# Another issuing queue for the MLP's right factors, and the last product's splits moved into the last chunk

## The chip, the cores and the metric

The kernel runs on one core of a Trainium2 chip. The metric is the device time of one execution in microseconds; of three executions the median counts.

## The reference, cut to what matters

The program is one step of a two-layer decoder trunk for 1024 prompt tokens and 8 single sample tokens (1032 columns), with width 1024 and an MLP width of 2816. Layer 0 mixes with GLA and NSA heads, layer 1 with an mLSTM; after either mixer comes the MLP, which is what the change is about:

```
for l in range(DEPTH):
    xp, xs = xp + mixer(rmsnorm(xp)), xs + mixer(rmsnorm(xs))
    # _conv_ffn(rmsnorm(x), w_up, conv_w, conv_b, w_down, conv_state):
    #   gate, inner = split(x @ w_up)             (1024 -> 2 x 2816)
    #   gate = causal depthwise conv of width 3 over gate, + bias
    #   d = (gelu_tanh(gate) * inner) @ w_down    (2816 -> 1024)
    xp, cv = xp + conv_ffn(xp), last two gate columns
    xs, cv = xs + conv_ffn(xs), the same with the state
y_prompt, y_sample = rmsnorm(xp), rmsnorm(xs)
```

All of it is float32.

## The kernel before, in words

**Products.** TensorE multiplies float32 operands as three products of halves: a high part (the value rounded to the engine's short float, ScalarE's copy) and a low part (the difference, VectorE's subtraction). A "split" below is this pair of instructions. The MLP saves multiplications by a scheme of 7 block products in place of 8: the left operand (weights) and the right operand (activations) are each combined into seven factors, and the seven results are added into four quarters. `seven` (L536) runs one such set; product `i` of a set is followed by `after(i, ...)`, which evicts it from its PSUM bank (`ppa`, `ppb`, `ppc` in turn).

**Left factors.** `factors` (L468) makes the seven left factors of a set: two weight loads issued on SyncE's queue (SP, L473), sums on GpSimd (POOL, L477 to L497), and per factor a high part and a PSUM copy on ScalarE (ACT, L485, L487) and a low part on VectorE (DVE, L488). `fill` keeps four factors made ahead of TensorE.

**Up-projection** (`climb`). 22 hidden blocks `f` of 128 columns; each is one `seven` of 24 matmuls a product. The evictions, convolution, GELU and gate of a block run on ScalarE, VectorE and GpSimd during the next blocks. Two neighbouring blocks are a pair, the right operand of the down-projection. When a pair is complete, `turn(f, i)` splits its seven combinations, one at a time (L738 high, next step L741 low), in two staging buffers in turn (named `st` and `big`; for layer 0's last pair slots 26 and 27, `s`), and a store (L742, SyncE's queue) of 516 KB sends each to the DRAM tile `hid`. A staging buffer is refilled when its store has landed.

**Down-projection** (`descend`). The pairs are taken in chunks: layer 0 has 11 pairs, in chunks of 2, 2, 2, 2 and 3; layer 1 has nine, in 2, 2, 2 and 3. A chunk runs four block rows `j`, each one `seven` of 12 matmuls a product (18 for three pairs). The chunk's right factors, seven per pair, come back from `hid` into slots (buffers `xh`, `xl`, `s`) by `load_factors` (L624), issued on ScalarE's queue: chunk 0's behind the first four products of the last up-projection block (L777 to L779), the next chunk's at the head of each `j` (L815), a third pair's at L828. In the last chunks the stored residual rows `res` come back on SyncE's queue (L839), are scaled (L841) and added (L843) by GpSimd. The rows themselves are stored by `out_project` (L419), on SyncE's queue, before the MLP begins.

**Last product.** Layer 1's pairs cover only blocks 0 to 17. Blocks 18 to 21 go unsplit to the DRAM tile `raw` (L712) and are multiplied plainly by `finish` (L888, matmuls at L902) after the last chunk: lines 598 to 612 load eight weight slices of 256 KB, split them (L273, L274 into `fh`, `fl`), load the four rows (L608) and split them (L609, L610), and then `finish` starts. It also makes the final norm and stores the results.

**What sets the order.** `plan(at, late, step)` puts a piece of work behind product number `at` of the whole run (`late` 0 is ahead of that step's `fill`, 1 behind it). `ordered` (L522) then holds TensorE, VectorE, ScalarE and GpSimd to the order in which the program emits their instructions, between the start of the up- and the end of the down-projection; SyncE is not among them. What is outside it, SyncE's DMAs included, is put in its queue by a planner, by its own estimate of when buffers come free. Each queue runs in its order, so an instruction that waits holds what is behind it.

Of the kernel before, what the change touches and what calls it, by code (L numbers as in the profile page):

```python
# [21 lines left out]
TT = T + NS  # L22
# [49 lines left out]
class Trunk:  # L72
# [304 lines left out]
    def out_project(self, l, w, split, ks, ready, late, nat=None):  # L377


        nc = self.nc  # L380
        with self.tp(name="opp", bufs=2, space=PSUM) as pp, \
                self.tp(name="opm", bufs=2, space=PSUM) as self.ps:
            oh, ol = [None] * KD, [None] * KD

            def parts(ids):
                for i in ids:
                    oh[i], ol[i] = split(ks[i])

            def begin(m):
                wt = self.split_w([(0, w[:, m * 128:(m + 1) * 128])], KD, nat=nat)  # L390
                pt = pp.tile([128, NG, 512], F32, name="pp")
                return pt, self.product_steps([pt[:, g, :GW] for g in range(NG)], wt, oh, ol, ks)

            parts(range(2))
            split2 = self.split
            parts(range(2, ready))
            head = [begin(PAIRS[0])]
            self.take(head[0][1], ready)
            head.append(begin(PAIRS[1]))
            for _ in range(ready):  # L400
                with self.tc.issue_after(split2):
                    next(late, None)
                self.take(head[1][1], 1)
            for _ in late:
                pass
            parts(range(ready, KD))
            self.res = self.dram.tile([KD, 128, TT], F32, name="res")
            self.right = [None] * 28
            for n, m in enumerate(PAIRS):
                pt, steps = head[n] if n < 2 else begin(m)  # L410
                self.take(steps, KD)
                x = self.rstd if n % 2 else self.vec.tile([128, TT], F32, name="sq_t")
                nc.gpsimd.tensor_tensor(x, self.xh[m].bitcast(F32), self.xl[m].bitcast(F32), op=OP.add)
                for g in ((slice(1, 3), slice(0, 1)) if n == KD - 1 else (slice(0, 3),)):
                    c = slice(g.start * GW, g.stop * GW)
                    v = x[:, c].rearrange("p (g t) -> p g t", t=GW)
                    nc.vector.tensor_tensor(v, pt[:, g, :GW], v, op=OP.add)
                    nc.scalar.activation(self.big[:, m, c], x[:, c], AF.Copy, scale=self.gains[:, 16 + 8 * l + m:17 + 8 * l + m])
                nc.sync.dma_start(self.res[m], x)  # L419
                nc.scalar.activation(x, x, AF.Square)  # L420
                self.add_sq(x, n)
                if n % 2:
                    self.prepare(n // 2)
# [145 lines left out]
    def ffn(self, l, last):  # L569
# [22 lines left out]
        with self.tp(name="fpp", bufs=1, space=PSUM) as pp, self.tp(name="fpm", bufs=2, space=PSUM) as self.ps:  # L592
            self.agenda, self.step = defaultdict(list), 0
            with self.ordered():
                self.climb(l, stream, pp, right, tu, chunks, hid, raw, NP)
                self.descend(l, last, stream, pp, tu, chunks, hid)
            assert not self.agenda
        while pools:
            pools.pop().__exit__(None, None, None)
        if last:  # L600
            with self.tp(name="fin", bufs=1) as fin:
                free = [self.slot(i).rearrange("p a q w -> p (a q w)") for i in (1, 3, 5, 7, 9, 11, 13)]
                wts = [self.last_weight(w_dn[18 * 128:], 4, m, fin) for m in range(KD)[::-1]][::-1]
                y, parts = [x.bitcast(F32) for x in free[:4]], free[4:]
                while len(parts) < 8:
                    parts.insert(3, fin.tile([128, TT], F32R, name=f"o{len(parts)}"))
                for k in range(4):
                    nc.sync.dma_start(y[k], raw[k])  # L608
                    nc.scalar.activation(parts[k], y[k], AF.Copy)  # L609
                    nc.vector.tensor_tensor(parts[4 + k], y[k], parts[k], op=OP.subtract)  # L610
                with self.tp(name="flp", bufs=8, space=PSUM) as self.ps:
                    self.finish(wts, parts[:4], parts[4:], y)
        else:
            self.open_x()
            self.order = PAIRS
            for n, m in enumerate(PAIRS):
# [4 lines left out]
                    nc.scalar.activation(x, big[:, PAIRS[n + 4]], AF.Square)  # L621
                    nc.vector.tensor_tensor(self.sq, self.sq, x, op=OP.add)

    def load_factors(self, p, at, hid, ids, eng):  # L624

        for i in ids:
            x = self.slot(at + 2 * i)
            eng.dma_start(x.bitcast(F32), hid[p, i])
            self.down[p, i] = x

    def climb(self, l, stream, pp, right, tmp, chunks, hid, raw, pairs):
# [17 lines left out]
        def up(f):  # L649
# [72 lines left out]
            if f >= 2 * pairs:  # L722
                self.plan(s + (4 if wide else 8), 0, keep)
            if f % 2 and f < 2 * pairs:
                for i, n in enumerate((5, 7, 9, 11, 12, 13, 14) if wide else (10, 12, 14, 16, 17, 18, 19)):
                    self.plan(s + n, 1, lambda i=i: turn(f, i))
            return after

# [2 lines left out]
        def turn(f, i):  # L731
# [7 lines left out]

            def low():  # L740
                v.tensor_tensor(to[:, 1, :, :QW], part, to[:, 0, :, :QW], op=OP.subtract)  # L741
                nc.sync.dma_start(hid[f // 2, MADE[i]], to.bitcast(F32))  # L742
                if i in (0, 2):
                    self.sums(1 if i == 0 else 4, src, p)
            self.plan(self.step + 1, 0, low)
# [26 lines left out]
        for f in range(NF):  # L772
            done = up(f)

            def after(i, pt):
                done(i, pt)
                if f == NF - 1 and i < 4:  # L777
                    for n, c in enumerate(chunks[0]):
                        self.load_factors(c, n, hid, range(2 * i, min(2 * i + 2, 7)), nc.scalar)  # L779

            self.seven(pp, stream, lambda i: right[4 * i:4 * i + 4], after)
        self.plan(self.step + 3, 1, lambda: self.conv_store(l, cvp, cvs, rows))

    def descend(self, l, last, stream, pp, tmp, chunks, hid):

        nc, big, v, p = self.nc, self.big, self.nc.vector, self.nc.gpsimd
        st = self.st.bitcast(F32).rearrange("p a q w -> p (a q w)")
# [20 lines left out]

        for c, chunk in enumerate(chunks):
            to_go = len(chunks) - 1 - c  # L810
            loads = [(x, 14 * (1 - c % 2) + n) for n, x in enumerate(chunks[c + 1][:2])] if to_go else []
            for j in range(4):
                a11, a12, a21, a22 = (x for m in (j, j + 4) for x in (big[:, m, :HW], big[:, m, HW:]))
                t = first[j]
                for x in loads:  # L815
                    self.load_factors(*x, hid, range(2 * j, min(2 * j + 2, 7)), nc.scalar)

                def after(i, pt):
                    to, k = ((t, None), (a12, None), (a22, None), (a11, left), (a22, right), (a12, right), (a21, left))[i]
# [5 lines left out]
                        x = (a22, a12, a21)[i]  # L825
                        p.tensor_tensor(x, x, t, op=OP.add)
                    if to_go == 1 and j == 3:
                        self.load_factors(chunks[-1][2], 14 * (c % 2), hid, (i,), nc.scalar)  # L828
# [38 lines left out]
    def conv_store(self, l, cvp, cvs, rows):  # L867
# [15 lines left out]
    def last_weight(self, w, n, m, pool):  # L883

        return self.part_w(self.load_w([(0, w[:, m * 128:(m + 1) * 128])], n),
                           to=[pool.tile([128, n, 128], F32R, name=f"{x}{m}") for x in ("fh", "fl")])

    def finish(self, wts, hh, hl, ys):  # L888

# [1430 lines left out]
```

## Time and profile before

| | |
|---|---|
| median of three runs | 2863.44 us (2860.78 to 2866.82) |
| profiled execution | 2869.35 us, its span 2867.6 us |
| mean granted TensorE clock | 0.973 of full speed |
| TensorE matmul | busy 2729.6 us, 95% of the span |
| VectorE, ScalarE, GpSimd | busy 64%, 47%, 38% |
| DMA | 341.51 MB, mean 119 GB/s; SyncE's queue has 24.2% of the sixteen engines' time, ScalarE's 7.7% |
| `hid` stores | 140 of 516 KB on SyncE's queue; as many loads on ScalarE's |

The up-projection of layer 0 runs to about 1350 us of the span, its down-projection from there on; layer 1's up-projection ends at about 2575, its last chunk begins at about 2717 and ends at 2786. In a row such as `ACT st L738 ... [6.67 <-DMA hid<-st]` the bracket is the idle time of the engine in front of the instruction and what ended it. `PE` is TensorE, `DVE` VectorE, `ACT` ScalarE, `POOL` GpSimd, `SP` SyncE; a `q` behind an engine's name is its sequencer issuing DMAs. A DMA share of 1 means that all sixteen DMA engines are busy.

### The profile page before, as it was taken

The page shows a single profiled execution, that of the slowest core. Times are in us where ns is not written, and L with a number is a line of the kernel's source. Part 1 is how long each engine was busy: PE and PEld are TensorE (multiplying, and loading weights), DVE is VectorE, ACT ScalarE, POOL GpSimd, SP SyncE. Part 2 cuts the span into 40 slices and gives each one's busy share as a digit, 9 for nine tenths or more (in the row PEclk, how much of TensorE's full clock was granted, in tenths as well). Part 3 has the DMA queues.
Part 4 walks back from the last instruction along what each step waited for, and adds up shares of the span by engine and source line. Part 5 has one row for each costly group of instructions (what it writes and reads, how often), then busy time and mean ns, then how long its engine had stood idle before and what let it go on. Part 6 is the DMA issues. An engine that isn't in the chain of part 4 may idle for free.

```text
span 2867.6 us, 49399 instructions
## 1 busy us (share of the span) xinstructions
PE 2729.6 (95%) x19507; PEld 2480.6 (87%) x19507; DVE 1846.7 (64%) x3080; ACT 1338.2 (47%) x2543; POOL 1093.7 (38%) x1025
## 2 busy tenths in 40 slices
PE   7999999999998999999899999999989999999988
PEld 7886544787798999999899889889989999999987
DVE  6556675447576777776576754444767777865664
ACT  4343444334345566665544422323455666645433
POOL 3531233331143455554375311110334545445713
PEclk9999999999898999999999999999999999999999
DMA  6620100541122334446785212221223343457711
GB/s 182 185 76 12 59 0 17 183 155 37 36 79 63 111 141 141 146 144 216 282 279 188 53 37 61 61 68 47 82 63 109 136 147 135 156 211 273 281 41 71
DMA packets 298347, 341.51 MB, mean 119 GB/s; under 512 B 33741, under 2 KB 245812, under 8 KB 298052
## 3 DMA queue, kind: packets, MB, share of 16 engines
q1 hardware_dynamic: 263356, 223.48, 24.2%
q10 hardware_dynamic: 25032, 81.32, 7.7%
q0 software_dynamic: 9728, 33.56, 3.4%
q8 instruction: 154, 2.52, 0.4%
q14 instruction: 77, 0.63, 0.1%
HBM read 240.56 MB, written 101.92 MB: 119 GB/s over the span
## 4 chain that ended last, share of the span: by engine, by line
PE 82%; DVE 7%; DMA 3%; ACT 3%; issue 2%; POOL 2%; ACTq 0%; SPq 0%; DVEq 0%; POOLq 0%
PE ppb L555 18%; PE ps L285 14%; PE ppa L555 11%; PE ppc L555 11%; PE pp L285 6%; PE ps L1425 2%; PE pd L285 2%; PE ps L902 2%; PE pd L1334 1%; PE ps L1182 1%; PE pd L1400 1%; PE ps L1170 1%; PE pd L1401 1%; PE ps L1580 1%; DMA wr<-in_ffn_w_down_dram 1%
## 5 line engine op out<-in xcount | busy, mean ns | idle before, releaser
L488 DVE TENSOR_TENSOR wh<-ps,wh 128x512 fp32r<-128x512 f32 (+2 forms) x280 | 162.3, 580 | 147.5 <-ACT ps L487 144.2
L488 DVE TENSOR_TENSOR wl<-ps,wl 128x512 fp32r<-128x512 f32 (+2 forms) x280 | 162.0, 578 | 100.9 <-ACT ps L487 97.5
L285 PE MATMUL ps<-xh,wh 128*128 128x344 f32 x960 | 223.9, 338 | 0.0
L285 PE MATMUL ps<-xl,wh 128*128 128x344 f32 x960 | 216.3, 329 | 4.4 <-DVE xl L188 2.5
L272 POOL TENSOR_TENSOR wr<-wr,gains 128x1024 f32<-128x1024 f32 (+1 forms) x44 | 85.0, 1933 | 335.0 <-DMA wr<-in_odd_w_in_dram 197.9
L285 PE MATMUL ps<-xh,wl 128*128 128x344 f32 x960 | 211.9, 326 | 0.0
L487 ACT COPY ps<-wr 128x512 f32<-128x512 f32 (+2 forms) x400 | 198.7, 497 | 7.6 <-DVE st L754 6.9
L555 PE MATMUL ppb<-s,wh 128*128 128x258 f32 x1380 | 183.5, 288 | 12.1 <-DVE sq L682 6.5
L555 PEld LDWEIGHTS ppb<-s,wh 128*128 128x128 f32 x1380 | 176.4, 195 | 12.8 <-ACT big L738 5.8
L555 PE MATMUL ppb<-s,wl 128*128 128x258 f32 x1380 | 179.2, 284 | 0.5 <-DVE sq_t L682 0.4
L493 POOL TENSOR_TENSOR wr<-wr,wr 128x512 f32<-128x512 f32 (+2 forms) x80 | 94.2, 1177 | 223.5 <-ACT ps L487 203.9
L285 PEld LDWEIGHTS ps<-xl,wh 128*128 128x128 f32 x960 | 164.9, 192 | 10.3 <-issue 4.5
L555 PEld LDWEIGHTS ppb<-s,wl 128*128 128x128 f32 x1380 | 171.9, 190 | 1.3 <-issue 0.9
L485 ACT ACTIVATE wh<-wr 128x512 fp32r<-128x512 f32 (+2 forms) x200 | 108.7, 544 | 135.7 <-PE ppb L555 54.6
L285 PEld LDWEIGHTS ps<-xh,wh 128*128 128x128 f32 x960 | 163.0, 192 | 6.5 <-issue 3.3
L285 PEld LDWEIGHTS ps<-xh,wl 128*128 128x128 f32 x960 | 164.7, 192 | 3.0 <-issue 2.6
L485 ACT ACTIVATE wl<-wr 128x512 fp32r<-128x512 f32 (+2 forms) x200 | 108.8, 544 | 123.5 <-PE ppb L555 55.6
L273 ACT ACTIVATE wh<-wr 128x1024 fp32r<-128x1024 f32 (+1 forms) x64 | 66.8, 1044 | 157.2 <-PE ps L285 107.9
L700 DVE SCALAR_TENSOR_TENSOR big<-big 128x524 f32<-128x524 f32 x176 | 130.6, 780 | 9.3 <-ACT big L697 9.2
L497 POOL TENSOR_TENSOR wr<-wr,s 128x512 f32<-128x512 f32 (+2 forms) x80 | 86.6, 1082 | 94.1 <-ACT ps L487 94.1
L1404 ACT ACTIVATE big<-pd 128x512 f32<-128x512 f32 x132 | 74.3, 597 | 93.4 <-PE pd L1401 54.1
L1341 DVE TENSOR_REDUCE m<-pd 128x1 f32<-128x512 f32 (+3 forms) x130 | 83.1, 661 | 49.4 <-PE pd L1339 38.6
(821 smaller groups left out, 7230.5 us busy)
## 6 DMA issues: line engine op xcount, KB each, us to landing
wr<-in_ffn_w_up_dram SPq DMA_DIRECT2D x88, 512.0 KB
hid<-big SPq DMA_DIRECT2D x67, 516.0 KB
hid<-st SPq DMA_DIRECT2D x66, 516.0 KB
s<-hid ACTq DMA_DIRECT2D x54, 516.0 KB
xh<-hid ACTq DMA_DIRECT2D x44, 516.0 KB
xl<-hid ACTq DMA_DIRECT2D x42, 516.0 KB
wr<-in_ffn_w_down_dram SPq DMA_DIRECT2D x64, 256.0 KB
wr<-in_odd_w_in_dram SPq DMA_DIRECT2D x24, 512.0 KB
```

Of the source, the lines that this page charges most:

```text
L272: self.gain_eng.tensor_tensor(raw, raw, gain[:, :, None].to_broadcast([128, kt, m]), op=OP.mult)
L273: nc.scalar.activation(wh, raw, AF.Copy)
L285: nc.tensor.matmul(outs[g], l[:, kw, :], r[k][:, g * GW:(g + 1) * GW], start=(n == 0 and i == 0), stop=(n == kt - 1 and i == 2))
L485: nc.scalar.activation(hi, x, AF.Copy)
L487: nc.scalar.copy(pt, x)
L488: nc.vector.tensor_tensor(lo, pt, hi, op=OP.subtract)
L493: nc.gpsimd.tensor_tensor(a11, a11, a21, op=OP.subtract)
L497: nc.gpsimd.tensor_tensor(a12, a12, s2, op=OP.subtract)
L555: nc.tensor.matmul(pt[:, q], w[:, k], r[:, part, q, :QW], start=(new and k == 0 and n == 0), stop=(k == len(right) - 1 and n == 2), skip_g ...
L700: v.scalar_tensor_tensor(cv[:, c], g[:, n + c.start:n + c.stop], taps[:, 22 * n + f:22 * n + f + 1], cv[:, c], op0=OP.mult, op1=OP.add)
L1341: nc.vector.tensor_reduce(m2[:, n, g, i0:i0 + hs, br], pt, AX.X, OP.max)
L1404: nc.scalar.activation(p[:, g * 512:(g + 1) * 512], pt, AF.Exp)
```

## The change

Five edits. (1) `load_factors` issues on SyncE's queue in place of ScalarE's. (2) `turn` stores a split on GpSimd's queue in place of SyncE's, at the end of the same step. (3) Layer 0's last pair is split at steps 8, 10, 12, 14, 16, 18, 20 behind its block, in place of 10, 12, 14, 16, 17, 18, 19. (4) Layer 1's last product is prepared by a new function, called at the head of the last chunk: its rows are loaded at once and split 10 to 14 products later, its weights come as four loads of 512 KB 19 and 25 products later; the weights' splits stand behind the chunk, in a pool that takes the memory of the slots 16 to 27. (5) The residual stores of the last two blocks of `out_project` go out on ScalarE's queue.

```diff
@@ out_project
-                nc.sync.dma_start(self.res[m], x)
+                (nc.sync if n < KD - 2 else nc.scalar).dma_start(self.res[m], x)
@@ ffn
-                self.descend(l, last, stream, pp, tu, chunks, hid)
+                self.descend(l, last, stream, pp, tu, chunks, hid, raw, w_dn[18 * 128:])
             assert not self.agenda
-        while pools:
-            pools.pop().__exit__(None, None, None)
+        pools.pop().__exit__(None, None, None)
         if last:
             with self.tp(name="fin", bufs=1) as fin:
...
+                y = [tu.rearrange("p a t -> p (a t)"), self.std] + [fin.tile([128, TT], F32, name=f"y{i}") for i in range(2)]
+                to = {m: [fin.tile([128, 4, 128], F32R, name=f"{x}{m}") for x in ("fh", "fl")] for m in range(KD)[::-1]}
+                hi, lo = self.last_right
+                lo.append(fin.tile([128, TT], F32R, name="ol"))
+                nc.vector.tensor_tensor(lo[3], self.last_x, hi[3], op=OP.subtract)
+                wts = [self.part_w(x, to=to[m]) for m, x in self.raws]
                 with self.tp(name="flp", bufs=8, space=PSUM) as self.ps:
-                    self.finish(wts, parts[:4], parts[4:], y)
+                    self.finish(wts, hi, lo, y)
@@ load_factors
-            eng.dma_start(x.bitcast(F32), hid[p, i])
+            self.nc.sync.dma_start(x.bitcast(F32), hid[p, i])
@@ climb
-                for i, n in enumerate((5, 7, 9, 11, 12, 13, 14) if wide else (10, 12, 14, 16, 17, 18, 19)):
+                for i, n in enumerate((5, 7, 9, 11, 12, 13, 14) if wide else (8, 10, 12, 14, 16, 18, 20)):
@@ turn, low
-                nc.sync.dma_start(hid[f // 2, MADE[i]], to.bitcast(F32))
+                self.plan(self.step, 1, lambda: p.dma_start(hid[f // 2, MADE[i]], to.bitcast(F32)))
@@ new
+    def last_product(self, raw, w, tmp):
+
+        nc, v = self.nc, self.nc.vector
+        flat = "p a q w -> p (a q w)"
+        free = [self.slot(i).rearrange(flat) for i in (1, 3, 5, 7, 9, 11, 13)]
+        hi, lo = free[:4], free[4:]
+        x = [tmp.rearrange("p a t -> p (a t)"), self.std] + [self.vec.tile([128, TT], F32, name=n) for n in ("sq_t", "sq")]
+        self.last_right, self.raws = (hi, lo), []
+        def high(k):
+            nc.scalar.activation(hi[k], x[k], AF.Copy)
+        def low(k):
+            if k == 3:
+                self.last_x = x[k]
+                return
+            v.tensor_tensor(lo[k], x[k], hi[k], op=OP.subtract)
+        def load(n):
+            x = (self.wraw if n % 2 else self.fx).tile([128, KD, 128], F32, name="wr" if n % 2 else "wr2", bufs=2)
+            x = x.rearrange("p (k a) m -> p k (a m)", k=4)
+            nc.sync.dma_start(x, w[:, n * 256:n * 256 + 256].rearrange("(k p) f -> p k f", p=128))
+            self.raws += [(2 * n + i, x[:, :, i * 128:i * 128 + 128]) for i in range(2)]
+        for k in range(4):
+            nc.sync.dma_start(x[k], raw[k])
+            self.plan(self.step + 10 + k, 1, lambda k=k: high(k))
+            self.plan(self.step + 11 + k, 0, lambda k=k: low(k))
+        for n in range(4):
+            self.plan(self.step + (19, 19, 25, 25)[n], 1, lambda n=n: load(n))
@@ descend, for each chunk
+            if last and not to_go:
+                self.last_product(raw, w_last, tmp)
```

## Rows read from the trace of the kernel before

**Rows 1.** Stretches: us, busy time (instructions) of each engine, PE clock, DMA share, GB/s

```profile
945.00:1320.00 375.00, 375.00 (x3117) 375.00 (x3116) 287.44 (x414) 228.91 (x397) 196.72 (x225) 1.00 0.40 140
1332.00:1356.00 24.00, 18.40 (x140) 18.22 (x139) 11.90 (x20) 9.59 (x19) 8.11 (x12) 0.86 1.01 370
1340.00:1420.00 80.00, 60.45 (x434) 59.11 (x433) 36.72 (x73) 41.83 (x103) 23.40 (x28) 0.87 0.82 293
1420.00:1600.00 180.00, 180.00 (x1501) 180.00 (x1500) 126.58 (x223) 88.35 (x223) 115.80 (x95) 1.00 0.62 212
2566.00:2622.00 56.00, 47.76 (x361) 47.22 (x360) 24.38 (x50) 31.29 (x80) 22.86 (x25) 0.91 0.83 294
2690.00:2722.00 32.00, 25.50 (x194) 24.94 (x193) 14.30 (x27) 12.82 (x32) 17.86 (x17) 0.89 0.88 320
2721.00:2785.00 64.00, 64.00 (x533) 64.00 (x533) 37.65 (x61) 22.70 (x49) 13.40 (x12) 1.00 0.12 34
2786.30:2802.50 16.20, 0.00 (x0) 0.00 (x0) 10.07 (x17) 5.18 (x8) 0.00 (x0) 0.59 0.33 97
2802.50:2806.30 3.80, 3.77 (x11) 3.54 (x12) 0.69 (x1) 0.00 (x0) 0.00 (x0) 0.50 0.00 0
2806.30:2825.00 18.70, 18.70 (x108) 18.70 (x108) 8.93 (x16) 4.20 (x8) 12.55 (x8) 1.00 0.00 1
```

**Rows 2.** Chain that ended last, 1330 to 1420: start us, us, what

```profile
1337.73 12.40 DMA xh<-hid
...
1350.19 8.98 DMA hid<-st
```

**Rows 3.** Timeline of TensorE, 1337 to 1420: start us, us, instructions [idle before <-releaser]

```profile
1352.07 4.71 PE L555 MATMUL ppb<-s,wh 128*128 128x258 f32 x24 [5.60 <-ACT big L738]
...
1371.06 0.38 PE L870 MATMUL ps<-ident,big 128*44 128x128 f32 x1 [5.72 <-DVE wl L488]
...
1399.91 2.84 PE L555 MATMUL ppb<-xl,wl 128*128 128x258 f32 x12 [2.87 <-DVE big L823]
```

**Rows 4.** Timeline of ScalarE and its queue, 1336 to 1370

```profile
1336.44 0.33 ACTq L628 DMA_DIRECT2D xl<-hid  x1
...
1337.73 7.27 ACTq L628 DMA_DIRECT2D xh<-hid  x4
1345.05 0.63 ACT L485 ACTIVATE wh<-wr 128x512 fp32r<-128x512 f32 x1 [7.10 <-DMA xl<-hid]
```

**Rows 5.** Chain that ended last, 2560 to 2620

```profile
2601.43 9.41 DMA wr<-in_ffn_w_down_dram
```

**Rows 6.** Timeline of SyncE's queue, 2590 to 2612

```profile
2601.43 5.72 SPq L473 DMA_DIRECT2D wr<-in_ffn_w_down_dram  x4
```

**Rows 7.** Chain that ended last, 2690 to 2830

```profile
2703.47 11.00 DMA xl<-raw
```

**Rows 8.** Timeline of TensorE, 2692 to 2722

```profile
2717.13 2.95 PE L555 MATMUL ppb<-xl,wl 128*128 128x258 f32 x12 [5.74 <-DVE big L823]
```

**Rows 9.** Groups by line, 2786 to 2803: busy us, mean ns, idle before <-releasers

```profile
L274 DVE TENSOR_TENSOR fl<-wr,fh 128x512 fp32r<-128x512 f32 x8 | 5.3, 686 | 6.1 <-ACT fh L273 5.9
L273 ACT ACTIVATE fh<-wr 128x512 fp32r<-128x512 f32 x8 | 4.9, 628 | 18.0 <-DMA wr<-in_ffn_w_down_dram 10.7 <-PE ppb L555 7.0
```

**Rows 10.** Waits, 945 to 1320: engine, line, waited for: us, times, longest

```profile
ACT st L738 <- DMA hid<-st: 7.5, 5, 2.4
...
SPq L742 <- DVE big L741: 121.3, 32, 11.4
```

**Rows 11.** Groups by line of VectorE and of GpSimd, 945 to 1320

```profile
L700 DVE SCALAR_TENSOR_TENSOR big<-big 128x524 f32<-128x524 f32 x75 | 54.4, 765 | 0.9 <-ACT big L697 0.8
...
L493 POOL TENSOR_TENSOR wr<-wr,wr 128x512 f32<-128x512 f32 x18 | 27.3, 1518 | 67.7 <-ACT ps L487 67.7
```

**Rows 12.** GpSimd's gather issues (line 1159): duration ns; then their idle time

```profile
L1159 POOL DMA_INDIRECT big<-in_cache_cmp_kv_dram,idx_cmp x32: 945/949/1797, 16.8 to 140.8; - x32
...
  issue: 11.8, 40
```

More of the change, by code (lines that the diff above doesn't have):

```diff
@@ L595, in ffn @@
                 self.climb(l, stream, pp, right, tu, chunks, hid, raw, NP)
-                self.descend(l, last, stream, pp, tu, chunks, hid)
+                self.descend(l, last, stream, pp, tu, chunks, hid, raw, w_dn[18 * 128:])
             assert not self.agenda
-        while pools:
-            pools.pop().__exit__(None, None, None)
+        pools.pop().__exit__(None, None, None)
         if last:
             with self.tp(name="fin", bufs=1) as fin:
[L602 to L610, printed above, removed]
+                y = [tu.rearrange("p a t -> p (a t)"), self.std] + [fin.tile([128, TT], F32, name=f"y{i}") for i in range(2)]
[4 more added lines that the diff above has]
+                wts = [self.part_w(x, to=to[m]) for m, x in self.raws]
                 with self.tp(name="flp", bufs=8, space=PSUM) as self.ps:
-                    self.finish(wts, parts[:4], parts[4:], y)
+                    self.finish(wts, hi, lo, y)
+            pools.pop().__exit__(None, None, None)
         else:
+            pools.pop().__exit__(None, None, None)
             self.open_x()
@@ L622, in ffn, with load_factors @@
                     nc.vector.tensor_tensor(self.sq, self.sq, x, op=OP.add)
-    def load_factors(self, p, at, hid, ids, eng):
+    def load_factors(self, p, at, hid, ids):
         for i in ids:
             x = self.slot(at + 2 * i)
-            eng.dma_start(x.bitcast(F32), hid[p, i])
+            self.nc.sync.dma_start(x.bitcast(F32), hid[p, i])
             self.down[p, i] = x
@@ L778, in after, with descend @@
                     for n, c in enumerate(chunks[0]):
-                        self.load_factors(c, n, hid, range(2 * i, min(2 * i + 2, 7)), nc.scalar)
+                        self.load_factors(c, n, hid, range(2 * i, min(2 * i + 2, 7)))
             self.seven(pp, stream, lambda i: right[4 * i:4 * i + 4], after)
         self.plan(self.step + 3, 1, lambda: self.conv_store(l, cvp, cvs, rows))
-    def descend(self, l, last, stream, pp, tmp, chunks, hid):
+    def last_product(self, raw, w, tmp):
[23 more added lines that the diff above has]
+            self.plan(self.step + (19, 19, 25, 25)[n], 1, lambda n=n: load(n))
+    def descend(self, l, last, stream, pp, tmp, chunks, hid, raw, w_last):
         nc, big, v, p = self.nc, self.big, self.nc.vector, self.nc.gpsimd
@@ L815, in descend @@
                 for x in loads:
-                    self.load_factors(*x, hid, range(2 * j, min(2 * j + 2, 7)), nc.scalar)
+                    self.load_factors(*x, hid, range(2 * j, min(2 * j + 2, 7)))
                 def after(i, pt):
@@ L827, in after @@
                     if to_go == 1 and j == 3:
-                        self.load_factors(chunks[-1][2], 14 * (c % 2), hid, (i,), nc.scalar)
+                        self.load_factors(chunks[-1][2], 14 * (c % 2), hid, (i,))
                     if not to_go:
@@ L881, in conv_store @@
             nc.sync.dma_start(d[i * 128:i * 128 + n], rows[:n, 1 + i])
-    def last_weight(self, w, n, m, pool):
-        return self.part_w(self.load_w([(0, w[:, m * 128:(m + 1) * 128])], n),
-                           to=[pool.tile([128, n, 128], F32R, name=f"{x}{m}") for x in ("fh", "fl")])
     def finish(self, wts, hh, hl, ys):
```

## The prediction

> **What bounds the kernel now.** I read the busy shares first (the table above): TensorE is busy 95% of the span, so only time in which it stands still can be won. The view by stretches says where that is. In the steady up-projection a matmul takes 375.00 / 3117 = 0.1203 us and there is no gap (945 to 1320) [rows 1]; the middle of the down-projection has none either (1420 to 1600) [rows 1]. For a stretch with gaps I take its length less its matmul count times 0.1203, which holds the idle time and the slow clock after it. Between layer 0's up- and down-projection (1340 to 1420) that is 80 - 434 x 0.1203 = 27.8 us; at the same place of layer 1 (2566 to 2622) 56 - 361 x 0.1203 = 12.6 us; at the head of layer 1's last chunk (2690 to 2722) 32 - 194 x 0.1203 = 8.7 us. Before the last product (2786.3 to 2806.3) there are 16.2 us without a matmul and then 11 matmuls in 3.8 us at a granted clock of 0.50, where the next stretch has 18.70 / 108 = 0.173 us each, so 1.9 us more: 18.1 us [rows 1]. Together 67.2 us, and all that this change can win. What ends the four stalls comes from the chain of waits and the timelines. In layer 0 the chain runs through transfers of right factors, in and out [rows 2], while the DMA engines are full: share 1.01 at 370 GB/s (1332 to 1356) [rows 1]. ScalarE, whose queue issues the loads, is held by them: one issue takes 0.33 us, but four together took 7.27, and the weight copy behind them started after 7.10 us idle [rows 4]. TensorE then stops 5.60, 5.72 and 2.87 us for split results [rows 3]. In layer 1 the chain has 9.41 us of a weight transfer, issued on SP's queue [rows 5, 6]; in the last chunk 11.00 us of the product's rows being loaded, then a stop of 5.74 us [rows 7, 8]; at the end the weight splits wait 18.0 us, 10.7 of it for weight loads [rows 9].
>
> **The change part by part.**
> *Last product inside the last chunk.* Today its rows and weights are loaded and split when the last chunk is over or, for the rows, in front of it. Now four weight loads of 512 KB go out 19 and 25 products into the chunk, where the DMA share is 0.12 (2721 to 2785) [rows 1]: 2.1 MB, 5.7 us at 370 GB/s, hidden. Added beside the matmuls are eight high parts of 0.628 us on ScalarE, eight low parts of 0.686 us on VectorE [rows 9], and three of the four row splits; ScalarE has 41 us idle in those 64 us, VectorE 26. What can still be late is the order on VectorE after the last product: the last eviction, the fourth row's low part and whatever of the eight low parts has not run. If all of these do, 5.3 us [rows 9], and the clock falls less than today; if none, one hop of about 0.3 us. The first group needs only the first block's parts, so I take 1.5 left: **-16.6 us** (-12.8 to -17.8).
> *The last chunk's rows.* The same 2.1 MB of rows now go to buffers that are free before the chunk's own loads, so they leave the queue ahead of that burst. The stop of 5.74 us was a weight split held in ScalarE's queue behind a row split whose transfer took 11.00 us [rows 7, 8]. The row splits now stand 10 products later, so this goes; late next are the third pair's loads in the same burst. I leave 2.5 of 8.7: **-6.2 us** (-2.7 to -8.7).
> *140 loads from ScalarE's queue to SP's, layer 1.* ScalarE no longer stalls on issues. But the weights come by SP too: four weight issues took 5.72 us there [rows 6], and the down-projection's weights will queue behind up to 14 loads of a chunk. 14 x 516 KB = 7.4 MB is 20 us at 370 GB/s (1.43 us each), and the seven products of a block row last 7 x 12 x 0.1203 = 10.1 us, with four factors ahead. So the stall at 2612, which ended with SP's weight transfer, need not go. I leave 8.6 of 12.6: **-4.0 us** (from 0 to -8; that the stall grows is counted under the next part's upper end).
> *The same, layer 0, with the stores.* The burst here is 28 loads of chunks 0 and 1, up to 13 stores of the last two pairs, ten weight loads and the residual rows: 41 x 0.528 + 2.6 + 1 = 25 MB, 68 us at 370 GB/s, against the 60 us that 1332 to 1420 would last without its 27.8. So about 8 us stay however it is issued. The other end: SyncE is not among the engines whose order is written down, so chunk 1's loads may be put in its queue early; a weight pair behind 28 loads lands 28 x 1.43 = 40 us after them, where the two block rows in front last 20, and with the slow clock after such a stop that is 24 left. I take the middle, 16 left: **-12 us** (-4 to -20). Spreading the last pair's splits (steps 8 to 20 in place of 10 to 19) puts a store into every second product; it serves this stop and has no term of its own.
> *Later chunks.* From 1420 on there are no gaps at a DMA share of 0.62 [rows 1], but loads that SP sends in a bunch can push weights back as above; 0 to 8 us, I take **+2**.
> *140 stores from SP's queue to GpSimd's.* The trace has no such store. The nearest row is GpSimd's gather issue, 0.949 us each [rows 12]; with 11.8 / 40 = 0.30 us of gap 1.25, so seven stores cost 8.8 us per pair of 2 x 7 x 24 x 0.1203 = 40.4 us. GpSimd is busy 196.72 of 375 us [rows 1], so 52% becomes 74%, and its longest wait there is for ScalarE, 67.7 us [rows 11]: room. In the steady stretch the splitting waits for a store only 7.5 us in five waits [rows 10], with no gap on TensorE. A store behind one GpSimd operation (1.5 us) and its own issue (0.95) leaves some 2.5 us later; VectorE's idle share (23%, 9.4 us per pair) and four factors ahead (11.6 us) take that up. **0** (0 to +60, rival D below; a gain is excluded as there is no gap to close).
> The Trainium skill, "SBUF — State Buffer", section "SBUF: two separate sides", speaks against this move: the descriptors of a transfer started by GpSimd are written by its own cores, which stand still while VectorE runs an operation that holds the shared port pair, and the same transfer from SP's queue would not. It names copies as the operation that does so; VectorE's costliest row of this stretch is a form with two tensor inputs [rows 11], so by the rule as well as by my term the price is near 0; were it to apply, it would be rival D below.
> *Four residual stores to ScalarE's queue* before the square there: 4 issues of 0.33 us [rows 4], partly in front of a norm; -0.5 to +2, I take **+0.5**.
> Sum: -16.6 - 6.2 - 4.0 - 12 + 2 + 0 + 0.5 = -36.3. The profiled execution took 2869.35 us, its span 2867.6 and 1.75 around it; it becomes 2833.0. It lies 5.9 above the median of the runs, 2863.44, from which the same step gives **2827 us**.
>
> **Rivals.**
> *The queue move works fully* (B). SP's stores waited for VectorE, 121.3 us in 32 waits of the steady stretch alone [rows 10], and held the weight loads behind them; with those gone weights come early, and only the volume bound stays. Left: 1.5 + 1 + 4 + 8 = 14.5 of 67.2, with +0.5: -52, **2811**. For it: the stops in rows 3 end with ScalarE's or VectorE's work, not with a load that TensorE itself needs. Against: share 1.01.
> *The stalls only change place* (C). At a full DMA the weights wait behind loads in SP's queue as the splits did in ScalarE's; only the finish is won, 18: **2845**. For it: rows 5 and 6, a stall that ends with SP's weight. A rule of the Trainium skill says as much, "DMA: Bandwidth & Descriptors", section "Issuing engines are not separate DMA queues": transfers of all issuing engines run on the same 16 DMA engines and interleave, and another issuer saves only the time of issuing. By it the sum would be this rival's; rows 4 agree only in part, since four issues held ScalarE for 7.27 us, which is not small.
> *Slower* (D). The place is the pair split in both up-projections. Two staging buffers are refilled only when a store has landed; on GpSimd each of seven stores leaves 2.5 us later, 17.5 us per pair, beyond the 11.6 of factors ahead, and TensorE stops. At 3 us in each of 20 pairs that is +60: 2863 - 36 + 60 = **2887**. It decides from 36 / 20 = 1.8 us per pair. For it: rows 10, the waits exist. Against: GpSimd and VectorE both have a quarter of the time free.
> *About as before* (E), the finish's gain given back in one of these places: **2860**.
>
> **How the numbers follow.** Forecast 0.45, B 0.25, C 0.18, D 0.07, E 0.05. The forecast's own range is 2812 to 2842 from its bounds. The range takes in B and C with some of their spread, 2804 to 2852; what is left out is D, E and the tails, 0.2 at most. A measurement of this kernel can tell about 0.2%, 5.7 us, from no change: faster A + B + C = 0.88, same 0.05, slower 0.07.
>
> **What would show it.** Finish: the first matmul of the last product within 5 us of the last chunk's end, at full clock. Last chunk: no stop before its first product. Layer 0: the stretch's excess falls to 8 to 24 us, and the stops that remain end with a weight copy waiting for SP's load; if instead they end with ScalarE's split waiting for a store, the queue of GpSimd is the cause. Climb: every stretch fully busy on TensorE, ScalarE's waits for stores longer than 7.5 us but without gaps. I am wrong if the finish still waits for weights, or if gaps appear in each pair.

## The result, and the profile after

The changed kernel is slower: 2880.91 us median (2875.98 to 2886.05) against 2863.44 (2860.78 to 2866.82), ratio 1.0061, 95% interval 1.0046 to 1.0077. The prediction was 2827 us, range 2804 to 2852, with 0.07 on slower: it was wrong.

The stretches of the profiled execution after (columns as in [rows 1]), the two up-projections, the two places behind them and the head of the last chunk:

```profile
945.00:1360.00 415.00, 395.44 (x3206) 392.62 (x3205) 307.83 (x428) 232.22 (x408) 233.60 (x290) 0.98 0.39 134
1360.00:1450.00 90.00, 69.48 (x522) 68.26 (x521) 45.94 (x84) 45.49 (x115) 33.81 (x46) 0.87 0.83 300
2185.00:2595.00 410.00, 391.46 (x3174) 388.67 (x3173) 300.93 (x419) 226.34 (x397) 231.15 (x289) 0.98 0.38 130
2595.00:2650.00 55.00, 52.02 (x431) 51.67 (x431) 33.52 (x62) 34.24 (x79) 24.68 (x30) 1.00 0.87 316
2716.00:2752.00 36.00, 35.66 (x295) 35.30 (x295) 23.27 (x44) 15.96 (x44) 30.60 (x27) 1.00 0.91 328
```

Length less matmul count times 0.1203 us, as in the prediction, gives the time lost: 415 - 3206 x 0.1203 = 29.3 us in layer 0's up-projection and 410 - 3174 x 0.1203 = 28.2 us in layer 1's, where there was none [rows 1]. Behind layer 0's it is 27.2 us (27.8 before), behind layer 1's 3.1 (12.6), at the last chunk's head 0.5 (8.7). The last product follows without a stop; its first gap, three us in, is 0.87 us:

```profile
2814.70 0.88 PE L555 MATMUL ppb<-xl,wh 128*128 128x258 f32 x6
2815.42 2.09 PE L928 MATMUL ps<-xh,fh 128*128 128x384 f32 x11
2818.38 0.44 PE L928 MATMUL ps<-xh,fl 128*128 128x384 f32 x1 [0.87 <-DVE fl L274]
```

So four places gave back some 35 us and two new ones took 57.5. That sums to +22, the medians differ by 17.5. The two spans differ by 11.6 only, since the part before the first MLP, which the change hardly touches, took some 7 us less in this execution; over the profiles of the first, second and last group of runs it varies from 876 to 885 us, with and without the change.

What stands still in the up-projections is shown by one pair. VectorE finishes a low part in the staging buffer `big`:

```profile
1110.45 0.68 DVE L739 TENSOR_TENSOR big<-big 128x516 fp32r<-128x516 f32 x1
...
1118.46 0.70 DVE L739 TENSOR_TENSOR big<-big 128x516 fp32r<-128x516 f32 x1 [4.91 <-ACT big L736]
```

GpSimd, whose queue has the store, is in `rest()` of the same block (L658 to L661) and comes to it at 1113.56, 2.43 us after the low part ended at 1111.13:

```profile
1110.61 1.68 POOL L658 TENSOR_TENSOR big<-tu,rstd 128x508 f32<-128x508 f32 x1 [1.85 <-DVE tu L682]
...
1113.56 0.59 POOL L740 DMA_DIRECT2D hid<-big  x1 [0.27 <-DVE wh L488]
```

ScalarE wants to split the next combination into that buffer and stands still until the store has landed; the weight splits of `fill` stand behind it in its queue:

```profile
1117.79 0.64 ACT L736 ACTIVATE big<-big 128x516 fp32r<-128x516 f32 x1 [6.22 <-DMA hid<-big]
```

VectorE's low part waited 4.91 us for it (1118.46 above), and TensorE has three gaps, 0.44 + 0.88 + 1.82 = 3.1 us, in this pair. Each ends with an eviction, not with a weight factor:

```profile
1118.95 3.15 PE L555 MATMUL ppa<-xl,wh 128*128 128x258 f32 x24 [0.44 <-ACT tu L666]
...
1125.87 3.12 PE L555 MATMUL ppc<-s,wh 128*128 128x258 f32 x24 [0.88 <-DVE big L673]
1130.81 3.15 PE L555 MATMUL ppb<-s,wl 128*128 128x258 f32 x24 [1.82 <-DVE big L680]
```

Over the stretch 945 to 1320 these waits of ScalarE were 7.5 us before [rows 10] and, for the other buffer,

```profile
ACT big L738 <- DMA hid<-big: 5.7, 4, 2.2
```

and are after

```profile
ACT st L736 <- DMA hid<-st: 28.9, 8, 7.5
ACT big L736 <- DMA hid<-big: 26.5, 10, 6.2
```

and VectorE's taps of the convolution, 765 ns each before [rows 11], are slower:

```profile
L698 DVE SCALAR_TENSOR_TENSOR big<-big 128x524 f32<-128x524 f32 x71 | 67.4, 988 | 4.5 <-ACT big L695 4.5
```

That left two candidates for the 57.5 us: **Q**, the store starts late in GpSimd's queue and the staging buffer is free too late; **P**, GpSimd's own sums are held behind the waiting store and then collide with VectorE's taps. A third, **L**, was that SyncE's queue with the loads is at fault, and a fourth, **G**, that a store by GpSimd as such is dearer, by a longer way to its landing for one.

### The profile page after: what moved, and what is told of

Read it like the earlier page. It is cut to its first block, busy times and chain, and to the rows that moved or that the text cites. A ratio compares the mean times of both kernels' runs of the same rounds, so it can differ in the third digit from the quotient of the medians.

```text
span 2879.2 us, 49474 instructions
## 1 busy us (share of the span) xinstructions
PE 2732.9 (95%) x19507; PEld 2477.7 (86%) x19507; DVE 1868.8 (65%) x3080; ACT 1332.7 (46%) x2543; POOL 1167.8 (41%) x1165
## 4 chain that ended last, share of the span: by engine, by line
PE 65%; DVE 16%; issue 6%; ACT 6%; DMA 4%; POOL 3%; SPq 0%; ACTq 0%; DVEq 0%; POOLq 0%
PE ps L285 14%; PE ppb L555 12%; PE ppa L555 6%; PE pp L285 6%; PE ppc L555 5%; DVE big L698 3%; PE pd L285 2%; PE ps L1451 2%; PE ps L928 2%; DMA hid<-st 1%; DMA hid<-big 1%; PE pd L1360 1%; DVE wh L488 1%; PE ps L1208 1%; PE ps L1196 1%
## 5 line engine op out<-in xcount | busy, mean ns | idle before, releaser
L555 PE MATMUL ppb<-s,wl 128*128 128x258 f32 x1380 | 189.7, 294 | 32.1 <-DVE sq_t L680 17.4
L555 PEld LDWEIGHTS ppb<-s,wl 128*128 128x128 f32 x1380 | 180.7, 200 | 36.3 <-ACT ps L487 35.2
L698 DVE SCALAR_TENSOR_TENSOR big<-big 128x524 f32<-128x524 f32 x176 | 163.5, 966 | 17.9 <-ACT big L695 17.9
L493 POOL TENSOR_TENSOR wr<-wr,wr 128x512 f32<-128x512 f32 (+2 forms) x80 | 86.7, 1084 | 141.0 <-ACT ps L487 130.8
```

The costliest lines, as they stand in the source:

```text
L493: nc.gpsimd.tensor_tensor(a11, a11, a21, op=OP.subtract)
L555: nc.tensor.matmul(pt[:, q], w[:, k], r[:, part, q, :QW], start=(new and k == 0 and n == 0), stop=(k == len(right) - 1 and n == 2), skip_g ...
L698: v.scalar_tensor_tensor(cv[:, c], g[:, n + c.start:n + c.stop], taps[:, 22 * n + f:22 * n + f + 1], cv[:, c], op0=OP.mult, op1=OP.add)
```

## The experiments

Runs of one group shared a chip and its runs of the kernel before; in the last group but one (free slots, spread for all pairs but one, only the loads) all kernels took longer (before: 2880.47), so ratios are compared.

**Stores back on SyncE's queue** (after, one edit).

```diff
-                self.plan(self.step, 1, lambda: p.dma_start(hid[f // 2, MADE[i]], to.bitcast(F32)))
+                nc.sync.dma_start(hid[f // 2, MADE[i]], to.bitcast(F32))
```

> The changed kernel with the hid stores back on SyncE's queue, issued right behind the low part; all else as changed. Theory Q (a store on GpSimd's queue starts late, behind GpSimd's sums of the same step, 1.77 us after the low part on the mean where SyncE took 0.04, and the split of the next combination waits for its staging buffer): the up-projections have no gaps again, both together 55 us less, so about 2881 - 55 = 2826 us; ScalarE's waits for stores in the stretch of nine pairs fall from 55 to about 13 us. Rival L (the loads on SyncE's queue, or the order the planner then gives it, cost the up-projections): they stay long, 2870 to 2885 us.

Measured 2813.86 us, ratio 0.9811 (0.9790 to 0.9832). The up-projection has no gap (385 us, 3200 matmuls); behind layer 0's 80 - 507 x 0.1203 = 19.0 us are left, behind layer 1's 1.0:

```profile
945.00:1330.00 385.00, 385.00 (x3200) 385.00 (x3200) 296.72 (x427) 234.71 (x409) 200.17 (x228) 1.00 0.41 142
1332.00:1412.00 80.00, 66.99 (x507) 66.12 (x506) 44.58 (x83) 45.39 (x113) 29.43 (x32) 0.87 0.93 329
...
2509.00:2565.00 56.00, 54.68 (x457) 54.51 (x455) 39.44 (x61) 32.47 (x63) 28.73 (x34) 1.00 0.70 260
```

ScalarE's waits for stores are back at 14 us:

```profile
ACT st L736 <- DMA hid<-st: 8.6, 5, 3.1
...
ACT big L736 <- DMA hid<-big: 5.3, 4, 1.8
```

L is out. The run is 67 us faster than the changed kernel, 12 more than expected, of which 8 lie behind layer 0's up-projection.

**Only the stores moved** (before, the same edit reversed).

> The kernel before with one edit: the hid stores on GpSimd's queue at the end of the step. Theory Q: both up-projections lose some 3 us a pair as in the changed kernel, 2863 + 55 = 2918 us. Rival L: no change in them, 2855 to 2870 us.

Measured 2926.27 us, ratio 1.0214 (1.0189 to 1.0239), +62.7 us; the up-projection loses 415 - 3183 x 0.1203 = 32.1 us:

```profile
945.00:1360.00 415.00, 393.06 (x3183) 389.91 (x3182) 304.08 (x424) 231.03 (x406) 234.10 (x288) 0.98 0.37 128
```

So the whole loss comes with this one edit.

**Stores on GpSimd's queue, but right behind the low part.**

```diff
-                self.plan(self.step, 1, lambda: p.dma_start(hid[f // 2, MADE[i]], to.bitcast(F32)))
+                p.dma_start(hid[f // 2, MADE[i]], to.bitcast(F32))
```

> The changed kernel with the hid stores on GpSimd's queue issued right behind the low part, ahead of the sums of that step. Theory Q: the store starts 0.3 to 0.5 us behind the low part, most of the 55 us comes back, 2826 to 2845 us, less what GpSimd's sums lose behind the waiting store. Rival G (what costs is a store by GpSimd as such: its longer way to the landing, or its descriptors beside VectorE's taps, which went from 765 to 988 ns): little comes back, 2865 to 2885 us.

Measured 2931.92 us, ratio 1.0237 (1.0215 to 1.0258): a miss, worse than the late store; the up-projection loses 445 - 3188 x 0.1203 = 61.5 us:

```profile
945.00:1390.00 445.00, 407.33 (x3188) 403.55 (x3187) 320.85 (x424) 231.68 (x405) 246.67 (x288) 0.95 0.37 123
```

The edit didn't do what I had meant. The store that matters comes behind L658 to L661, which GpSimd has in its queue before the low part is emitted: it still started at 1028.91, 2.42 us after its low part, and the others now make GpSimd wait (2.03 us at 1020.51) ahead of its sums:

```profile
1020.51 0.57 POOL L740 DMA_DIRECT2D hid<-st  x1 [2.03 <-DVE st L739]
...
1028.91 0.58 POOL L740 DMA_DIRECT2D hid<-big  x1 [0.27 <-DVE wh L488]
```

So this run decided nothing between Q and P. Nor is its doubled loss explained: ScalarE's waits for stores in 945 to 1320 come to 52.8 us, no more than the 55.4 of the changed kernel:

```profile
ACT st L736 <- DMA hid<-st: 29.0, 5, 8.2
...
ACT big L736 <- DMA hid<-big: 23.8, 4, 7.3
```

**What is left without the loads and stores moved** (after).

```diff
-                self.plan(self.step, 1, lambda: p.dma_start(hid[f // 2, MADE[i]], to.bitcast(F32)))
+                nc.sync.dma_start(hid[f // 2, MADE[i]], to.bitcast(F32))
-            self.nc.sync.dma_start(x.bitcast(F32), hid[p, i])
+            self.nc.scalar.dma_start(x.bitcast(F32), hid[p, i])
```

> The changed kernel with loads back on ScalarE's queue and stores back on SyncE's: what is left of the change is the last product inside the last chunk, the spread of layer 0's last pair and four residual stores on ScalarE's queue. Expected: the last product's 17 us and the last chunk's 8 us are won, the stalls between up- and down-projection stand as before (27.8 and 12.6 us): 2863 - 25 = 2838 us. If the last product's gain hangs on the loads' queue: 2845 to 2860.

Measured 2833.6 us, ratio 0.9887 (0.9866 to 0.9908). Left are 80 - 428 x 0.1203 = 28.5 us behind layer 0's up-projection, 11.5 behind layer 1's, 1.1 at the last chunk's head:

```profile
1330.00:1410.00 80.00, 60.23 (x428) 58.98 (x428) 38.83 (x72) 41.83 (x100) 24.19 (x30) 0.87 0.87 312
2550.00:2606.00 56.00, 47.80 (x370) 47.26 (x369) 27.31 (x54) 29.09 (x72) 16.44 (x19) 0.93 0.86 310
2674.00:2706.00 32.00, 31.20 (x257) 30.84 (x257) 19.59 (x40) 13.49 (x39) 23.91 (x22) 1.00 1.00 359
```

**The splits spread** (after; each staging buffer is refilled four products later).

```diff
-                for i, n in enumerate((5, 7, 9, 11, 12, 13, 14) if wide else (8, 10, 12, 14, 16, 18, 20)):
+                for i, n in enumerate((5, 7, 9, 11, 13, 15, 17) if wide else (8, 10, 12, 14, 16, 18, 20)):
```

> The changed kernel with the pair splits of the up-projection in every second product (steps 5, 7, 9, 11, 13, 15, 17 in place of 5, 7, 9, 11, 12, 13, 14): each staging buffer has four products, 11.6 us, until it is filled again, so no split waits for a store. Theory Q (the split waits for a staging buffer whose store starts late on GpSimd's queue): most of the 58 us of both up-projections comes back, 2825 to 2840 us. Rival P (the store, waiting in GpSimd's queue for the low part, holds GpSimd's own sums, which then run beside VectorE's taps; those take 988 ns in place of 765): the waits for stores vanish and the time stays, 2865 to 2885 us.

Measured 2814.35 us, ratio 0.9834 (0.9816 to 0.9852). In layer 0's last pair but one the late splits read rows that the down-projection has begun to overwrite, so this kernel's output is not the program's; the instructions are the same, and only its time is used. The up-projection is whole (385 - 3193 x 0.1203 = 0.9 us), with the stores on GpSimd's queue:

```profile
945.00:1330.00 385.00, 384.68 (x3193) 384.37 (x3193) 311.23 (x425) 235.35 (x406) 223.60 (x290) 1.00 0.39 138
```

The waits for stores are gone, but for

```profile
ACT big L736 <- DMA hid<-big: 1.7, 1, 1.7
```

and the taps are as slow as in the changed kernel and cost nothing:

```profile
L698 DVE SCALAR_TENSOR_TENSOR big<-big 128x524 f32<-128x524 f32 x76 | 74.0, 1012 | 0.0
```

That is Q, and against P's collision. It is against G too: GpSimd issues the same stores here and no time is lost. The landing did not change much either: from issue to landing the stores took 3.2 to 3.3 us (median, by their semaphores' updates) on SyncE's queue before and 3.2 to 3.4 after, in the stretch 945 to 1320 3.4 and 3.8 on the mean, while the start moved by 1.8.

**A copy on GpSimd in the store's place** (stores on SyncE's queue; the copy puts 200 columns of the low part into a tile `idle` that nobody reads).

```diff
                 nc.sync.dma_start(hid[f // 2, MADE[i]], to.bitcast(F32))
+                self.plan(self.step, 1, lambda: p.tensor_copy(self.idle, to.bitcast(F32)[:, 1, 0, :self.idle.shape[1]]))
```

> The stores on SyncE's queue as in the run of 2814 us, and in the place of the store on GpSimd a copy of 200 columns of the low part into a tile that nobody reads: GpSimd waits for the low part as it did for the store, but no staging buffer waits for GpSimd's queue for long. Theory P: the up-projections lose 30 us or more again, 2845 to 2875 us. Theory Q: at most 10 us, 2812 to 2825 us.

Measured 2810.84 us, ratio 0.9820 (0.9798 to 0.9842): 63 copies of some 0.47 us, each waiting for the low part as the store did, and no gap:

```profile
945.00:1330.00 385.00, 385.00 (x3200) 385.00 (x3199) 289.25 (x426) 235.01 (x408) 217.45 (x294) 1.00 0.41 138
```

```profile
L742 POOL COPY idle<-big 128x200 f32<-128x200 f32 x32 | 15.1, 472 | 20.5 <-DVE big L740 20.3
```

So GpSimd's wait alone costs nothing at the old steps; it had the room that the prediction gave it. The taps took 826 ns here, so this run has P's wait with little of its collision, and the run with the spread has the collision without the old steps. P is out as the main cause. A small part of it isn't excluded: at the gaps that end with L673, 2.1 of TensorE's 19.6 us of idle time in the changed kernel's stretch 945 to 1360, VectorE had worked through from the slow taps.

**Layer 0's stall: four slots for the last pair** (stores on SyncE's queue).

```diff
-            to = stage[staged % 2] if f < NF - 1 else self.slot(26 + staged % 2)
+            to = stage[staged % 2] if f < NF - 1 else self.slot((24, 25, 26, 27, 26, 27, 26)[i])
-                if f == NF - 1 and i < 4:
+                if f == NF - 1:
-                        self.load_factors(c, n, hid, range(2 * i, min(2 * i + 2, 7)))
+                        self.load_factors(c, n, hid, (i,))
```

> The run of 2814 us (stores on SyncE's queue) with two edits for layer 0's stall: the last pair is staged in four slots in place of two, so its splits do not wait for the store before last, and chunk 0's loads are given out two per product over seven products in place of four over four. Where the stall is the staging (the chain has 4.75 and 7.28 us of such stores): 3 to 8 us less, 2806 to 2811. Where it is the volume of the burst: unchanged, 2811 to 2816.

Measured 2817.55 us, ratio 0.9843 (0.9824 to 0.9862): no gain that can be told. In its trace 80 - 517 x 0.1203 = 17.8 us are left behind layer 0's up-projection, of 19.0.

**The last pair at its old steps** (stores on SyncE's queue).

```diff
-                ... if wide else (8, 10, 12, 14, 16, 18, 20)):
+                ... if wide else (10, 12, 14, 16, 17, 18, 19)):
```

> The run of 2814 us with the last pair's splits at the old steps 10, 12, 14, 16, 17, 18, 19. If the spread helps the stall of layer 0: 2 to 6 us more, 2816 to 2820. If not: 2814 within 2.

Measured 2816.06 us, ratio 0.9846 (0.9828 to 0.9863). What the spread of the last pair is worth is less than these times resolve. In this run's trace 80 - 482 x 0.1203 = 22.0 us are left behind layer 0's up-projection, 3 more than with the spread, which is within the first expectation.

**Free slots for the last two pairs** (on top of the run with four slots).

```diff
-            to = stage[staged % 2] if f < NF - 1 else self.slot((24, 25, 26, 27, 26, 27, 26)[i])
+            if f == NF - 1 or (f == NF - 3 and i > 2):
+                to = self.slot((24, 25, 26, 27, 26, 27, 26)[i] if f == NF - 1 else (14, 15, 16, 20)[i - 3])
+            else:
+                to = stage[staged % 2]
```

> The run of 2814 us (stores on SyncE's queue) with layer 0's last two pairs staged in slots that stand free: the last pair in slots 24 to 27, and the last four splits of the pair before it in slots 14, 15, 16 and 20, which the up-projection's last block has just left. No split there waits for a store. Theory Q, for layer 0's stall too: of the 19 us that are left of it (7.36 and 3.47 us of stop and the slow clock behind them) some 8 to 12 go, 2802 to 2807 us. If the volume of the burst holds it: 2811 to 2816.

Measured 2831.71 us beside 2880.47, ratio 0.9818 (0.9795 to 0.9842), as without the edit. The stop of 7.36 us is gone, and 80 - 529 x 0.1203 = 16.4 of 19.0 us are left:

```profile
1352.00:1432.00 80.00, 67.87 (x529) 66.91 (x528) 47.71 (x87) 46.35 (x116) 29.20 (x32) 0.94 0.97 337
```

```profile
1390.12 1.69 PE L555 MATMUL ppb<-xl,wh 128*128 128x258 f32 x12 [2.77 <-DVE big L857]
...
1398.04 2.95 PE L555 MATMUL ppb<-xh,wh 128*128 128x258 f32 x12 [4.79 <-ACT big L855]
```

Other waits in that stretch took its place, for weights and for the last pair's stores, at a DMA share of 0.97:

```profile
POOL s L477 <- DMA wr<-in_ffn_w_down_dram: 12.4, 3, 10.2
...
ACT s L739 <- DMA hid<-s: 3.9, 1, 3.9
```

**The spread for all pairs but one** (after).

```diff
-                ... ((5, 7, 9, 11, 12, 13, 14) if wide else ...
+                ... ((5, 7, 9, 11, 12, 13, 14) if f == NF - 3 else (5, 7, 9, 11, 13, 15, 17) if wide else ...
```

> The changed kernel, stores on GpSimd's queue, with the spread steps 5, 7, 9, 11, 13, 15, 17 for every pair of the up-projections but layer 0's last but one, which keeps the old steps. Theory Q: as the run with the spread alone, 2812 to 2822 us; VectorE's taps stay near 1000 ns and cost nothing.

Measured 2842.61 beside 2880.47, ratio 0.9863 (0.9840 to 0.9885). The up-projection loses 375 - 3102 x 0.1203 = 1.8 us; behind layer 0's, 90 - 532 x 0.1203 = 26.0 us are left, as in the changed kernel, where the spread of all pairs had left 80 - 510 x 0.1203 = 18.6 (the last row is of that run):

```profile
945.00:1320.00 375.00, 373.87 (x3102) 373.38 (x3101) 301.66 (x412) 227.97 (x392) 218.23 (x284) 1.00 0.39 134
```

```profile
1355.00:1445.00 90.00, 69.58 (x532) 68.53 (x531) 46.79 (x84) 44.72 (x112) 32.84 (x46) 0.89 0.84 296
```

```profile
1337.00:1417.00 80.00, 65.97 (x510) 65.02 (x509) 45.71 (x83) 44.72 (x111) 32.69 (x44) 0.91 0.90 326
```

So the one pair with the old steps, beside the burst of loads, makes 7.4 us there.

**Only the loads moved** (before).

```diff
     def load_factors(self, p, at, hid, ids, eng):
+        eng = self.nc.sync
```

> The kernel before with one edit: the hid loads on SyncE's queue. From the difference of two earlier runs (2833.6 with the loads on ScalarE's queue, 2813.9 on SyncE's): both stalls between up- and down-projection lose some 10 us, 2863 - 20 = 2843 us. If the loads' gain needs the other edits (free rows, spread): 2850 to 2865.

Measured 2857.69 beside 2880.47, ratio 0.9914 (0.9891 to 0.9937), -23 us. Left are 22.4 us behind layer 0's up-projection, 1.1 behind layer 1's and none at the last chunk's head:

```profile
1356.00:1436.00 80.00, 63.45 (x479) 62.59 (x478) 42.75 (x78) 43.83 (x109) 27.13 (x31) 0.85 0.90 324
2576.00:2632.00 56.00, 54.69 (x456) 54.51 (x455) 30.55 (x62) 36.09 (x94) 31.99 (x31) 1.00 0.96 350
2700.00:2732.00 32.00, 32.00 (x267) 32.00 (x267) 19.09 (x33) 15.72 (x33) 14.97 (x14) 1.00 0.67 232
```

**Early stores and the spread together** (the earlier miss, spread for all pairs but one).

```diff
+                p.dma_start(hid[f // 2, MADE[i]], to.bitcast(F32))
+                ... ((5, 7, 9, 11, 12, 13, 14) if f == NF - 3 else (5, 7, 9, 11, 13, 15, 17) if wide else ...
```

> The stores on GpSimd's queue right behind the low part, as in the run of 2932 us, with the spread steps for every pair but layer 0's last but one. If that run's other 60 us came from GpSimd's sums held behind the waiting store, a spread doesn't free them: the up-projections still lose 30 us or more, a ratio to the kernel before of 1.00 or above. If they too came from the reuse of the staging buffers: as the run with the spread and late stores, a ratio of 0.985 to 0.99.

Measured 2818.82 us, ratio 0.9855 (0.9830 to 0.9881); 385 - 3166 x 0.1203 = 4.1 us lost in place of 61.5:

```profile
945.00:1330.00 385.00, 382.71 (x3166) 381.29 (x3165) 315.67 (x425) 232.92 (x403) 234.89 (x287) 1.00 0.41 138
```

GpSimd waited for low parts even longer than in the earlier miss (91 us in 945 to 1320, 62 there), and 4.1 us were lost. So those waits alone do not cost the 61.5; the loss needs the close refills. Which part of it is the staging buffers and which the sums, held in four consecutive products, this run doesn't part: the spread gives room to both.

## Why the prediction was wrong

**The stores: the step that failed.** "VectorE's idle share ... and four factors ahead ... take that up. 0 (0 to +60 ...)". The delay was sized about right (2.5 us forecast; 2.43 us in the pair shown, 1.8 on the mean of all stores in the profile after, where SyncE took 0.04), and GpSimd's time is no issue. The cover failed. The last four of the seven splits stand in consecutive products, 2.9 us apart, with two buffers, so the program fills a buffer again after 5.8 us. In layer 0's first ten pairs the two closest refills of a pair came 7.0 us after the fill on the mean before, and 10.3 after. From a low part to the next fill of its buffer the changed kernel takes 2.43 + 4.23 = 6.7 us in the pair shown. The wait falls on ScalarE, whose queue also makes the weights: idle time of VectorE doesn't help it. Nor do four factors ahead: all 19.6 us of TensorE's idle time in 945 to 1360 (of 29.3 lost; the rest is matmuls that took longer behind the stops) end with an eviction, 15.1 of them with that of a block's fifth product:

```profile
PE ppb L555 <- DVE sq_t L680: 8.4, 5, 1.9
PE ppb L555 <- DVE big L680: 6.7, 4, 1.9
```

In the pair shown this eviction stands in VectorE's queue behind the low part of a weight, which waited 1.09 us for ScalarE. The existing waits of [rows 10], 13 us with the other buffer's and without a gap, were read as room; they showed that this loop had no slack left.

Rival D had the place and the wait, and +60 against 57.5 measured; its chance of 0.07 was too low. That the price came so near is partly luck: 3 us a pair was set and not worked out, and its seven delays that add up to 17.5 us are not what happened, since only the fills in consecutive products wait longer.

The Trainium skill, "SBUF — State Buffer", section "SBUF: two separate sides", pointed to the same edit for another reason, that VectorE can keep GpSimd from writing a transfer's descriptors. The runs don't bear that out as the cause: with the spread GpSimd issued the same stores beside the same operations of VectorE, they landed after 3.0 us (median in 945 to 1320), and no time was lost.

**Last product: right.** -16.6 forecast; 18.1 us before, about 1 after, and the same gap of 0.87 us in the run with the loads back on ScalarE's queue.

**The last chunk's head: right in size (-6.2, measured -8.2), only half right in cause.** The prediction had the weight split held behind a row split. In the trace before, the row splits (L609) come behind it. What stands ahead of it is the issue of a load, and that waits until the rows' transfer (11.00 us, [rows 7]) has landed, at 2714.47:

```profile
2714.55 0.33 ACTq L628 DMA_DIRECT2D xh<-hid  x1
2714.98 0.52 ACT L485 ACTIVATE wl<-s 128x384 fp32r<-128x384 f32 x1 [5.94 <-DMA xl<-raw]
...
2716.65 2.01 ACT L609 ACTIVATE xh<-xh 128x1032 fp32r<-128x1032 f32 x2
```

So either edit takes the stop away. With ScalarE's loads in place the earlier rows do it (1.1 us left); with only the loads moved, and the rows as before, it goes too. Together they don't add.

**Loads, layer 1: right in sign, too small.** -4.0 forecast, 12.6 to 1.0 measured. The weights queued behind loads on SyncE's queue, which I had left 8.6 us for, arrived in time. **Layer 0:** -12 forecast, -0.6 measured in the changed kernel, -8.8 with the stores on SyncE's queue; the loads alone made -5.4 (27.8 to 22.4), and the spread of the last pair, which the prediction gave no term, some 3. The forecast counted the stores' volume and not their lateness, which takes the 8 us back. What then remains, 16 to 19 us, stayed through four slots, free slots and other orders; the volume of the burst (68 us of transfers for 60, worked out before) fits 8 of it, the rest is open.

**Rivals B and C.** Rival B's 2811 us was reached with the stores still on SyncE's queue, so its reason, that they hold the weight loads there, wasn't needed. The rule that rival C took from the Trainium skill ("DMA: Bandwidth & Descriptors", section "Issuing engines are not separate DMA queues"), that another issuing engine saves only issuing time, would have left the loads' move at nothing; alone it won 23 us beside its own runs of the kernel before. What it saves is not the issue but the work queued behind it: the weight split of [rows 4] waited 7.10 us behind four issues. The prediction took the 7.27 us for the issues' own time. In the trace each takes 0.33 us, and the other 6 us or so are waits. The DMAs of SyncE's and ScalarE's queues share eight completion semaphores in this kernel, and each of the four issues starts within 0.1 us of the landing of an earlier DMA on its own semaphore, the last of them after a landing at 1344.60:

```profile
1344.68 0.33 ACTq L628 DMA_DIRECT2D xh<-hid  x1
```

On SyncE's queue such a wait holds other transfers, but no compute.

**The version that beats both.** Everything of the change but the stores, 2813.86 us, ratio 0.9811; with the free slots the ratio is 0.9818, the same within the intervals.

## What to carry to other kernels

A transfer that frees a buffer belongs on a queue that has nothing else to do at that moment; moving it behind compute adds that compute to the buffer's turn. Before such a move, add up the whole turn (fill, store, landing, refill) against the time between refills, and look at who else is in the waiting engine's queue; small waits without gaps in a double buffer are a warning, not room. An engine that computes pays for a DMA that it issues with the waits ahead of the issue, not only with the issue. If the queue can't be chosen, spacing the refills evenly gave most of the time back here (0.9863 with all pairs spread but one, 0.9811 with the stores on SyncE's queue); the source rows must then live as long.

## What the runs showed of the hardware

A 516 KB store issued by GpSimd held it 0.56 us, less than the 0.949 us of the gather issue that I had taken, and landed 3.2 to 3.4 us after its issue (page after; the last column is us to landing):

```profile
hid<-big POOLq DMA_DIRECT2D x67, 516.0 KB, 3.2
hid<-st POOLq DMA_DIRECT2D x66, 516.0 KB, 3.4
```

On SyncE's queue before, an issue took 0.32 us and the landing 3.2 to 3.3 us.

The taps, which read two tensors in SBUF, went from 766 ns with the stores on SyncE's queue to 826 with the copies on GpSimd and 975 to 1265 with the stores there, without any change to them. The Trainium skill, "SBUF — State Buffer", section "SBUF: two separate sides", says that such an operation and one of GpSimd that reads SBUF hold a shared port pair in turn; the prediction had taken from this section only what it says of copies. The numbers fit the rule, but no run here took GpSimd's operations away to show it.
